# A hand-written order of TensorE's work in an attention stage, five probability row buffers and a shorter mask

## The chip, the cores and the metric

The kernel runs on one core of one Trainium2 chip. The metric is the device time of one execution in microseconds (us). Before the change it is 913.64 us, the median of three runs (912.99 to 913.8). The four engines that matter here are TensorE (PE in the rows, its weight loads PEld), VectorE (DVE), ScalarE (ACT) and SyncE (SP), which issues the DMAs.

## What is computed

A trunk of two layers over 1040 tokens (1024 frames behind 16 meta tokens), width 1024: first multi-head latent attention, then a gated linear recurrence, each with an output projection and a residual, and a last norm. The change touches the attention alone. Cut to what matters, for each of 8 heads:

```
s = (q_nope @ k_nope.T + q_rope @ k_rope.T) * scale     # 1040 x 1040
s = where(key <= query, s, -1e30)
p = softmax(s, axis=-1)
o = p @ v                                               # 1040 x 128
y = o * silu(gate)
```

All matrices are 32-bit. Each operand is split into a high and a low part (`hi_of` on ACT, `lo_of` on DVE), and a product is three matmuls: high by high, high by low, low by high (`mm3`).

## The kernel before, in words

**The stages.** The input norm, the latent projections, the gates and the rotary part of the queries come first. Then comes the attention (lines 420 to 699), from about 202 to 513 us of the span, then the output projection, the recurrence and its projection.

**The units of the attention.** Queries are cut into nine blocks of 116 rows (the last has 112), `QBLK`, line 43. A unit is one head and one block (h, t), and there are 72 of them. Three blocks make a group of 348 queries, `CH`. For each unit the program does the following, in this order.

- `scores(h, t)`, line 485: five matmuls for each piece of up to 512 keys, into a PSUM tile of two banks, `ps_2`. Block 0 to 2 have one piece, block 3 has one of 464 keys, blocks 4 to 7 have two, and block 8 has three (two in a first tile and one in a second one). There are two such tiles. Then DVE adds the mask and takes the row's minimum `m` (line 515, the queries carry the minus sign), ACT does the exponential into the row buffer `p` and the row's sum `l` (line 523), DVE the reciprocal (line 527), and DVE or, from block 6 on, ACT scales the row (lines 528 to 531). For block 8 the minimum is taken over both tiles (line 521) before either exponential.
- `transposes(h, t)`, line 534: TensorE transposes the row, 116 keys at a time, up to three into one PSUM tile `pt` (there are two of these, `nt[0] = 2`); ACT makes the high part `pth` of it (line 80) and DVE the low part `ptl` (line 83).
- `weighted(h, g)`, line 560: once for each group of three blocks, the transposed rows times `v`, into a PSUM tile of `ps_g`, and DVE multiplies by the gate into `Y` (line 574).

The k, q and v products of the coming head (`k_unit`, `q_unit`, `v_unit`) and the loads and splits of the next weights (`load_pair`, `part_out`) are handed out to units by the table `fill` (line 648 on). In the last head the places of the coming head's work are taken by the first tiles of the output projection (`part_out`, `a_out0`).

**What sets the order.** A main loop (line 686) records `scores` three units ahead (`LEAD = 3`), then `weighted`, then the unit's `fill`, then `transposes`. The recording is no order of execution: a scheduler orders each engine's instructions from its own plan of the time, and each engine then works through its list strictly in turn. So a row of transposes may stand in the middle of another product. `behind(marks, f)` holds f's instructions behind the given ones.

**Buffers.** Row buffers `p` are three of 1040 columns (line 496). The mask is 8 x 116 columns, zero but for a triangle at its end (line 424). [...]

**Names below.** s2_8_1 are the scores of head 2, block 8, tile 1; pt2_6_1 the second PSUM tile of transposes of head 2, block 6; o2_1 the weighted product of head 2, group 1; pk, pqn and pv the products of `k_unit`, `q_unit`, `v_unit`; kh, qh, wah, yh are high parts (ACT) and kl, ql, wal, yl low parts (DVE) of keys, queries, output weights and attention outputs; ao0_0 the first tile of the output projection. In ptl7_0_0 the numbers are head, group and tile, so its source tells the block.

Of the kernel before, what the change touches and what calls it, by code (L numbers as in the profile page):

```python
# [47 lines left out]
MASKW = 8 * QB  # L48
# [14 lines left out]
def trunk(ctx, tc, x, meta, a_norm_g, a_w_in, a_q_g, a_kv_g, a_w_uq, a_w_ukv, a_w_out,  # L63
# [20 lines left out]

    def mm3(ps, lh, ll, rh, rl, start, stop, **kw):
        nc.tensor.matmul(ps, lh, rh, start=start, stop=False, **kw)  # L86
        nc.tensor.matmul(ps, lh, rl, start=False, stop=False, **kw)  # L87
        return nc.tensor.matmul(ps, ll, rh, start=False, stop=stop, **kw)  # L88

    def mm_stack(ps, xp, k, n, wh, wl):  # L90
        if k:
            nc.tensor.matmul(ps[:n], xp[:, k, :n], wl, start=False, stop=False)
        nc.tensor.matmul(ps[:STK + n], xp[:, k], wh, start=k == 0, stop=k == KT - 1)
        if not k:
            nc.tensor.matmul(ps[:n], xp[:, k, :n], wl, start=False, stop=False)
# [41 lines left out]
    def rms_r(ms, n, w, name):  # L137
        v = sml.tile([P, w], F32, name=f"v_{name}", tag="rv")[:n]
        r = sml.tile([P, w], F32, name=f"r_{name}", tag="rr")[:n]
        t = sml.tile([P, w], F32, name=f"t_{name}", tag="rt")[:n]  # L140
        root = nc.scalar.activation(t, ms, AF.Sqrt, bias=eps[:n])
        nc.vector.tensor_scalar(v, ms, -0.5, -0.5 * EPS, ALU.mult, ALU.add)
        nc.vector.reciprocal(t, t)
        if w == 1:
            nc.vector.scalar_tensor_tensor(r, t, v, t, ALU.mult, ALU.mult)
        else:
            nc.vector.tensor_tensor(r, t, t, ALU.mult)
            nc.vector.tensor_tensor(r, r, v, ALU.mult)
        nc.vector.scalar_tensor_tensor(r, r, 1.5, t, ALU.add, ALU.mult)
        return r, root  # L150
# [16 lines left out]
    def transpose_in(xn, n, t0, xth, xtl, name):  # L167
        for j in range(2):
            pt = ps_t(f"xt_{name}_{j}")
            pv = pt.rearrange("p (a b) -> p a b", b=P)[:, :, :n]  # L170
            for a in range(4):
                k = 4 * j + a
                nc.tensor.transpose(pv[:, a], xn[:n, k * P:(k + 1) * P], ident[:n, :n])
# [97 lines left out]
    def lat_norm(i, pq, pk):  # L271
        t0, n = TOK[i]
        ms = sml.tile([P, 2], F32, name=f"lms{i}", tag="lms")[:n]
# [20 lines left out]
    def lat_post(i, lt, krf):  # L294
# [3 lines left out]
        for a in range(QKT):  # L298
            nc.tensor.transpose(pv[:, a], lt[:, a * P:(a + 1) * P], ident[:n, :n])
        nc.tensor.transpose(pv[:, 3], krf[:, 0:P], ident[:n, :n])  # L300
# [5 lines left out]
        for a in range(VKT):  # L306
            nc.tensor.transpose(pv[:, a], lt[:, QL + a * P:QL + (a + 1) * P], ident[:n, :n])
        nc.tensor.transpose(pv[:, 2], krf[:, DR:DR + P], ident[:n, :n])
# [19 lines left out]
    for c in range(0, D, 512):  # L328
        ps = ps_m(f"rb_ga{c}")
        nc.tensor.matmul(ps, ones, g_a[0:1, c:c + 512], start=True, stop=True)  # L330
# [98 lines left out]

    def load_pair(h):  # L430
# [10 lines left out]
    def k_unit(h, c):  # L441
# [6 lines left out]
        for k in range(VKT):  # L448
            last = mm3(ps, kvw[0][:, k, hh * 256:hh * 256 + DN], kvw[1][:, k, hh * 256:hh * 256 + DN],
                       klh[:, k, c0:c0 + cw], kll[:, k, c0:c0 + cw], k == 0, k == VKT - 1)  # L450
        kh, kl = KK[h]
        hi_of(kh[:, c0:c0 + cw], ps)
        lo_of(kl[:, c0:c0 + cw], ps, kh[:, c0:c0 + cw])
        return last
# [30 lines left out]
    def scores(h, t):  # L485
# [10 lines left out]
        p = pat.tile([QB, T], F32, name=f"p{h}_{t}", tag="p", bufs=3)[:n]  # L496
        pss = []
        a, b_, r_ = qh[:, off:off + n], ql[:, off:off + n], qr[:, off:off + n]
        for s, sg in enumerate(tiles):
            ps2 = ps_2(f"s{h}_{t}_{s}")  # L500
            w = sg[0][1]
            for j, (k0, w_) in enumerate(sg):
                assert w_ == w
                ps = ps2[:n, j, :w]
                nc.tensor.matmul(ps, a, kth[:, k0:k0 + w], start=True, stop=False)  # L505
                nc.tensor.matmul(ps, a, ktl[:, k0:k0 + w], start=False, stop=False)
                nc.tensor.matmul(ps, b_, kth[:, k0:k0 + w], start=False, stop=False)
                nc.tensor.matmul(ps, r_, ks1[:, k0:k0 + w], start=False, stop=False)
                nc.tensor.matmul(ps, r_, ks2[:, k0:k0 + w], start=False, stop=True)  # L509
            ns, k0 = len(sg), sg[0][0]  # L510
            pv = ps2[:n, :ns, :w]
            if s == len(tiles) - 1:
                lo = MASKW - QB - (ns * w - n)
                mk = maskt[:n, lo:lo + ns * w].rearrange("p (a b) -> p a b", a=ns)
# [3 lines left out]
            pss.append((pv, p[:, k0:k0 + ns * w].rearrange("p (a b) -> p a b", a=ns)))  # L518
        mx = m[:, 0:1]
# [14 lines left out]
    def transposes(h, t):  # L534
# [3 lines left out]
        p = PP.pop((h, t))  # L538
        if t % 3 == 0:
# [3 lines left out]
        for tr in range(g + 1):  # L543
# [4 lines left out]
            for j, kb in enumerate(kbs):  # L548
                k0, nk = QBLK[kb]
                nc.tensor.transpose(pv[:nk, j], p[:, k0:k0 + nk], ident[:n, :n])  # L550
# [98 lines left out]
    for h in range(H):  # L649
        for c in range(len(CH)):  # L650
# [3 lines left out]
            if u + 1 >= 0:  # L654
                fill[units[u + 1]].append(lambda h=h, c=c: q_unit(h, c))
# [15 lines left out]
    behind([silu], nc.scalar.activation, warm, ones[:, 0:1], AF.Exp)  # L671
    k_unit(0, 0)
    ku = k_unit(0, 1)
    behind([ku], q_unit, 0, 0)
    for u in range(-LEAD - 2, 0):
        for c in (1, 2):
            if 3 * c - LEAD - 2 == u and c > 1:
# [6 lines left out]
    for u in range(LEAD):  # L684
        scores(*units[u])
    for u, (h, t) in enumerate(units):
        if u + LEAD < len(units):
            scores(*units[u + LEAD])
        if pending:
            weighted(*pending)  # L690
            pending = None
        for f in fill[h, t]:
            f()
        transposes(h, t)
        if t % 3 == 2:
            pending = (h, t // 3)
    weighted(*pending)
# [299 lines left out]
    def late(i, c, done):  # L997
        ms = sml.tile([P, 1], F32, name=f"msb{i}", tag="msb", bufs=2)
        square(i, c, ms)
        v = sml.tile([P, 1], F32, name=f"v_f{i}", tag="rv")  # L1000
# [143 lines left out]
```

## Time and profile before

| | |
|---|---|
| median of three runs | 913.64 us |
| the profiled execution, its own time | 913.04 us |
| its span | 911.3 us |
| TensorE busy | 887.8 us, 97% of the span, 5291 matmuls |
| VectorE busy | 582.9 us, 64% |
| ScalarE busy | 467.7 us, 51% |
| GpSimd busy | 43.6 us, 5% |
| mean granted clock of TensorE | 0.997 |
| chain that ended last | TensorE 92%, ScalarE 3%, VectorE 2% |

A matmul's row is as long as it takes from its start to its end, and the next one starts before that end; so "busy" hides the spacing of starts, and a pause between two matmuls shows as idle time only from the end of the first.

### The profile page before, as it was taken

The numbers are of one execution on the slowest core, as the hardware profiler recorded it, in microseconds if no ns is written. First come the engines' busy times: TensorE is split into PE (matmuls) and PEld (weight loads), VectorE is DVE, ScalarE is ACT, GpSimd is POOL, SyncE is SP. The second block draws the span as 40 slices with busy tenths as digits, with TensorE's granted clock in tenths as the row PEclk, the third lists the DMA queues.
The fourth block names the chain that finished last, engine by engine and source line by source line (L and its number), as shares of the span: only waits on it lengthen the run. The fifth ranks groups of instructions, "written<-read, shape, count | busy, mean of one in ns | idle before, by whom it ended". The sixth has DMA issues, their size and how long they took to land.

```text
span 911.3 us, 13708 instructions
## 1 busy us (share of the span) xinstructions
PE 887.8 (97%) x5291; PEld 817.2 (90%) x5291; DVE 582.9 (64%) x1211; ACT 467.7 (51%) x942; POOL 43.6 (5%) x46
## 2 busy tenths in 40 slices
PE   7999999999999999999999999999999999999996
PEld 5999999999999999999988778799989989897885
DVE  6675423416677676676777357757393764868997
ACT  6543422224665655656656235634835457365455
POOL 3000000000000000000000000000020110312200
PEclk9999999999999999999999999999999999999998
DMA  7132345221010010010012424241111121237624
GB/s 275 48 87 64 85 110 158 73 72 40 16 57 16 17 55 16 17 63 16 17 37 103 163 92 159 101 75 48 46 47 51 43 58 36 95 90 231 141 68 184
DMA packets 71169, 72.25 MB, mean 79 GB/s; under 512 B 15056, under 2 KB 52688, under 8 KB 71104
## 3 DMA queue, kind: packets, MB, share of 16 engines
q1 hardware_dynamic: 68928, 67.19, 23.8%
q0 software_dynamic: 2176, 4.19, 2.6%
q8 instruction: 41, 0.67, 0.3%
q14 instruction: 24, 0.20, 0.1%
HBM read 58.65 MB, written 12.71 MB: 78 GB/s over the span
## 4 chain that ended last, share of the span: by engine, by line
PE 92%; ACT 3%; DVE 2%; issue 1%; DMA 0%; ACTq 0%; DVEq 0%
PE pt L550 4%; PE pu L88 3%; PE pu L86 3%; PE pu L87 3%; PE ga L86 3%; PE ao L86 3%; PE ga L87 3%; PE ga L88 3%; PE ao L88 3%; PE ao L87 3%; PE pg L87 3%; PE pg L88 3%; PE pg L86 3%; PE s L505 2%; PE b L86 2%; PE b L88 2%
## 5 line engine op out<-in xcount | busy, mean ns | idle before, releaser
L523 ACT ACTIVATE p<-s,m 116x116 f32<-116x116 f32 (+4 forms) x80 | 55.4, 694 | 45.1 <-DVE m L515 16.5
L80 ACT ACTIVATE pth<-pt 116x348 fp32r<-116x348 f32 (+5 forms) x152 | 57.1, 397 | 29.7 <-PE pt L550 26.2
L83 DVE TENSOR_TENSOR ptl<-pt,pth 116x348 fp32r<-116x348 f32 (+5 forms) x152 | 63.7, 437 | 9.7 <-ACT pth L80 9.2
L88 PE MATMUL pu<-x2h,l_wu 128*128 128x348 f32 (+1 forms) x192 | 61.5, 321 | 0.4 <-DVE l_wu L83 0.4
L86 PE MATMUL ga<-xth,h_wg 128*128 128x348 f32 (+1 forms) x192 | 61.9, 322 | 0.0
L86 PE MATMUL pu<-x2h,h_wu 128*128 128x348 f32 (+1 forms) x192 | 61.7, 322 | 0.0
L87 PE MATMUL pu<-x2l,h_wu 128*128 128x348 f32 (+1 forms) x192 | 61.7, 321 | 0.0
L87 PE MATMUL ga<-xtl,h_wg 128*128 128x348 f32 (+1 forms) x192 | 61.6, 321 | 0.0
L88 PE MATMUL ga<-xth,l_wg 128*128 128x348 f32 (+1 forms) x192 | 61.6, 321 | 0.0
L515 DVE CUSTOM_DVE_ANT_0 s<-s,maskt 116x116 f32<-116x116 f32 (+8 forms) x72 | 49.4, 686 | 16.9 <-PE s L509 16.6
L550 PE MATMUL pt<-ident,p 116*116 116x116 f32 (+1 forms) x360 | 54.0, 262 | 1.0 <-DVE ptl L83 0.6
L86 PE MATMUL ao<-wah,yh_a 128*128 128x512 f32 x128 | 50.5, 396 | 0.6 <-DVE Y L574 0.6
L87 PE MATMUL pg<-x2l,h_wbg 128*128 128x512 f32 x128 | 50.6, 395 | 0.0
L88 PE MATMUL pg<-x2h,l_wbg 128*128 128x512 f32 x128 | 50.3, 393 | 0.0
L86 PE MATMUL pg<-x2h,h_wbg 128*128 128x512 f32 x128 | 50.2, 392 | 0.0
L88 PE MATMUL ao<-wah,yl_a 128*128 128x512 f32 x128 | 50.2, 393 | 0.0
L87 PE MATMUL ao<-wal,yh_a 128*128 128x512 f32 x128 | 49.8, 390 | 0.0
L505 PE MATMUL s<-kh,qh 128*116 128x348 f32 (+7 forms) x120 | 42.0, 350 | 6.5 <-ACT p L523 6.5
L550 PEld LDWEIGHTS pt<-ident,p 116*116 116x116 f32 (+1 forms) x360 | 41.5, 135 | 4.0 <-PE pt L550 1.5
L87 PE MATMUL o<-ptl,v 116*128 116x348 f32 (+1 forms) x144 | 45.1, 313 | 0.0
L86 PE MATMUL o<-pth,v 116*128 116x348 f32 (+1 forms) x144 | 43.2, 300 | 0.8 <-ACT pth L80 0.8
L88 PE MATMUL o<-pth,v 116*128 116x348 f32 (+1 forms) x144 | 44.0, 305 | 0.0
(328 smaller groups left out, 2652.7 us busy)
## 6 DMA issues: line engine op xcount, KB each, us to landing
wg<-in_a_w_in SPq DMA_DIRECT2D x8, 512.0 KB, 3.9
wa<-in_a_w_out SPq DMA_DIRECT2D x8, 512.0 KB, 3.5
wu<-in_b_w_in SPq DMA_DIRECT2D x8, 512.0 KB, 4.0
wbg<-in_b_w_in SPq DMA_DIRECT2D x8, 512.0 KB, 4.0
hr<-hscr SPq DMA_DIRECT2D x8, 512.0 KB, 8.2
out_h<-hr SPq DMA_DIRECT2D x16, 256.0 KB, 2.1
x<-in_x SPq DMA_DIRECT2D x7, 512.0 KB, 3.5
wq<-in_b_w_out SPq DMA_DIRECT2D x6, 512.0 KB, 3.5
```

Source lines behind the costliest of these rows:

```text
L80: return nc.scalar.activation(dst, src, AF.Copy)
L83: return nc.vector.tensor_tensor(dst, src, bc(hi), ALU.subtract)
L86: nc.tensor.matmul(ps, lh, rh, start=start, stop=False, **kw)
L87: nc.tensor.matmul(ps, lh, rl, start=False, stop=False, **kw)
L88: return nc.tensor.matmul(ps, ll, rh, start=False, stop=stop, **kw)
L505: nc.tensor.matmul(ps, a, kth[:, k0:k0 + w], start=True, stop=False)
L515: MKD[h, t] = nc.vector.tensor_tensor_reduce(pv, pv, mk, 1.0, -NEG, ALU.add, ALU.min, m[:, s:s + 1])
L523: MK[h, t] = nc.scalar.activation(dst, pv, AF.Exp, bias=mx, scale=-1.0, accum_out=l[:, s:s + 1])
L550: nc.tensor.transpose(pv[:nk, j], p[:, k0:k0 + nk], ident[:n, :n])
```

## The change

In steps: (1) all of TensorE's instructions are issued through `pe_mm` and `pe_tr`, which keep the last one in `PE_LAST`; in the main loop every step is held behind it (`next_pe`), so that in the attention TensorE's list is the recorded order. (2) That order is: the first tile's scores of the unit three ahead; the third tile of transposes of the unit before (`back`, only of blocks 6 to 8); the weighted product that is pending; the unit's `fill`; the second tile's scores and the softmax; the first two tiles of transposes of this unit. `scores` is a generator for this, which stops between its tiles. In `fill`, `q_unit` goes to the front of its list. (3) The row buffers become five, of their own widths, by the table `PSLOT`. (4) The mask becomes 5 x 116 columns, read for several pieces with overlap (`mask_of`). (5) At the start, the first `k_unit` is followed by the first `q_unit` and only then by the second `k_unit`, and the table of the exponential is loaded behind the first high part of the keys. (6) Some buffers of single columns become two instead of four.

```diff
-MASKW = 8 * QB
+MASKW = 5 * QB
+PSLOT = (0, 1, 2, 3, 4, 1, 2, 3, 4)
...
+    PE_LAST = [None]
+
+    def pe_mm(*a, **kw):
+        PE_LAST[0] = nc.tensor.matmul(*a, **kw)
+        return PE_LAST[0]
...
-        v = sml.tile([P, w], F32, name=f"v_{name}", tag="rv")[:n]
+        v = sml.tile([P, w], F32, name=f"v_{name}", tag="rv", bufs=2)[:n]
...
+    def mask_of(n, ns, w):
+        m = maskt[:n, MASKW - QB - (w - n) - (ns - 1) * n:]
+        return bass.AP(m.tensor, m.offset, [m.ap[0], (n, ns), (1, w)])
...
-        p = pat.tile([QB, T], F32, name=f"p{h}_{t}", tag="p", bufs=3)[:n]
+        sl = PSLOT[t]
+        pw = max(QBLK[u][0] + QBLK[u][1] for u in range(NQB) if PSLOT[u] == sl)
+        p = pat.tile([QB, pw], F32, name=f"p{h}_{t}", tag=f"p{sl}", bufs=1)[:n]
...
             pss.append((pv, p[:, k0:k0 + ns * w].rearrange("p (a b) -> p a b", a=ns)))
+            if s + 1 < len(tiles):
+                yield
...
-    def transposes(h, t):
+    def transposes(h, t, trs):
...
-                fill[units[u + 1]].append(lambda h=h, c=c: q_unit(h, c))
+                fill[units[u + 1]].insert(0, lambda h=h, c=c: q_unit(h, c))
...
-    behind([silu], nc.scalar.activation, warm, ones[:, 0:1], AF.Exp)
-    k_unit(0, 0)
-    ku = k_unit(0, 1)
-    behind([ku], q_unit, 0, 0)
+    first_k = behind([silu], k_unit, 0, 0)
+    behind([first_k], nc.scalar.activation, warm, ones[:, 0:1], AF.Exp)
+    q_unit(0, 0)
...
+    def next_pe(f, *a):
+        behind([PE_LAST[0]], f, *a)
+
+    back = None
     for u, (h, t) in enumerate(units):
-        if u + LEAD < len(units):
-            scores(*units[u + LEAD])
+        sc = scores(*units[u + LEAD]) if u + LEAD < len(units) else iter(())
+        next_pe(next, sc, None)
+        if back:
+            next_pe(transposes, *back)
+            back = None
         if pending:
-            weighted(*pending)
+            next_pe(weighted, *pending)
             pending = None
+        end = u + 1 == len(units)
+        if end:
+            next_pe(transposes, h, t, range(2))
         for f in fill[h, t]:
-            f()
-        transposes(h, t)
+            next_pe(f)
+        next_pe(next, sc, None)
+        if not end:
+            next_pe(transposes, h, t, range(min(t // 3 + 1, 2)))
+        if t // 3 == 2:
+            back = (h, t, (2,))
         if t % 3 == 2:
             pending = (h, t // 3)
```

**TensorE where one head's scores pass to the next head's**, here from head 2 to head 3 (six such places follow the same pattern, one with each next head). Before, with 18 rows of o2_1 and six of pv1_7 between:

```order
L509 MATMUL s2_8_1_3450<-ks2_87,qr2_2_3324 112x344
L550 MATMUL pt2_6_0_3530<-ident_78,p2_6_3344 116x116
L550 MATMUL pt2_6_1_3536<-ident_78,p2_6_3344 116x116 x3
L86 MATMUL o2_1_3504<-pth2_1_0_3371,v1_0_3094 128x348
...
L88 MATMUL pv1_7_3559<-h_wkv2_2929,kll_94 116x256
L550 MATMUL pt2_6_2_3542<-ident_78,p2_6_3344 116x116
L505 MATMUL s3_0_0_3494<-kh3_3413,qh3_0_3473 116x116
```

and now:

```order
L89 MATMUL s2_8_1_3466<-ks2_87,qr2_2_3324 112x344
L93 MATMUL pt2_5_0_3479<-ident_78,p2_5_3294 116x116 x3
L93 MATMUL pt2_5_1_3485<-ident_78,p2_5_3294 116x116 x3
L89 MATMUL s3_0_0_3494<-kh3_3413,qh3_0_3460 116x116
...
L89 MATMUL o2_1_3504<-pth2_1_0_3371,v1_0_3094 128x348
...
L93 MATMUL pt2_6_0_3530<-ident_78,p2_6_3344 116x116 x3
L93 MATMUL pt2_6_1_3536<-ident_78,p2_6_3344 116x116 x3
L89 MATMUL s3_1_0_3545<-kh3_3413,qh3_0_3460 116x232
...
L93 MATMUL pt2_6_2_3555<-ident_78,p2_6_3344 116x116
```

The next head's first scores have moved up: between them and the last scores of this head stand six transposes, where four transposes, 18 matmuls of o2_1, six of pv1_7 and one more transpose stood.

**VectorE in the last head**, from the low part of the last queries on. Before:

```order
L586 TENSOR_TENSOR wal0_0_5629<-wa0_0_5626,wah0_0_5628 128x1024
L586 TENSOR_TENSOR wal0_1_5635<-wa0_1_5632,wah0_1_5634 128x1024
L515 ISA s7_6_0_5593,m7_6_5590<-s7_6_0_5593,maskt_2172 116x2x406
...
L83 TENSOR_TENSOR yl_a0_0_0_5726<-Y_1217,yh_a0_0_0_5725 128x512
L527 RECIPROCAL l7_5_5551<-l7_5_5551 116x1
L83 TENSOR_TENSOR ptl7_0_0_5513<-pt7_2_0_5584,pth7_0_0_5512 116x3x116
L586 TENSOR_TENSOR wal0_2_5641<-wa0_2_5638,wah0_2_5640 128x1024
```

and now:

```order
L604 TENSOR_TENSOR wal0_0_5629<-wa0_0_5626,wah0_0_5628 128x1024
L604 TENSOR_TENSOR wal0_1_5635<-wa0_1_5632,wah0_1_5634 128x1024
L531 ISA s7_6_0_5593,m7_6_5590<-s7_6_0_5593,maskt_2172 116x2x406
...
L545 RECIPROCAL l7_5_5551<-l7_5_5551 116x1
L604 TENSOR_TENSOR wal0_2_5641<-wa0_2_5638,wah0_2_5640 128x1024
L84 TENSOR_TENSOR ptl7_0_0_5513<-pt7_2_0_5584,pth7_0_0_5512 116x3x116
```

A third split of output weights now stands ahead of the low part of block 2's transposes, and one of the outputs (yl) has gone behind it. **TensorE** there, from the last scores of block 6 on, before:

```order
L509 MATMUL s7_6_0_5593<-ks2_87,qr7_2_5582 116x406
L505 MATMUL s7_7_0_5667<-kh7_5229,qh7_2_5578 116x464
...
L86 MATMUL o7_0_5608<-pth7_0_0_5512,v3_0_4910 128x348
L86 MATMUL ao0_0_5724<-wah0_0_5628,yh_a0_0_0_5725 128x512
...
L87 MATMUL o7_0_5608<-ptl7_0_0_5513,v3_0_4910 128x348
```

and now:

```order
L89 MATMUL s7_6_0_5593<-ks2_87,qr7_2_5582 116x406
L89 MATMUL o7_0_5608<-pth7_0_0_5512,v3_0_4910 128x348
L89 MATMUL o7_0_5608<-ptl7_0_0_5513,v3_0_4910 128x348
...
L93 MATMUL pt7_3_0_5654<-ident_78,p7_3_5464 116x116 x3
...
L89 MATMUL s7_7_0_5667<-kh7_5229,qh7_2_5578 116x464
```

The weighted product o7_0, whose second matmul reads that low part, follows block 6's scores at once, where ten matmuls of block 7's scores and twelve of ao0_0 stood between.

## Rows read from the trace of the kernel before

**Rows 1.** The page, busy time of the engines.

```profile
PE 887.8 (97%) x5291; PEld 817.2 (90%) x5291; DVE 582.9 (64%) x1211; ACT 467.7 (51%) x942; POOL 43.6 (5%) x46
```

**Rows 2.** Busy time by stretch: us, busy us of PE, PEld, DVE, ACT, POOL, clock, DMA.

```profile
202.00:215.00 13.00, 11.35 (x80) 10.88 (x79) 6.72 (x22) 7.14 (x18) 0.00 (x0) 1.00 0.30 84
215.00:470.00 255.00, 249.01 (x1739) 240.40 (x1738) 178.70 (x494) 150.39 (x378) 0.00 (x0) 1.00 0.09 28
470.00:515.00 45.00, 42.02 (x238) 36.09 (x237) 28.41 (x59) 23.48 (x47) 0.20 (x1) 1.00 0.30 107
```

**Rows 3.** PE's waits from 202 to 515: us in total, times, longest.

```profile
PE s L505 <- ACT p L523: 6.5, 9, 1.0
```

**Rows 4.** Timeline in head 1: start, us, engine, line, operation, [idle before <-releaser].

```profile
264.44 0.94 ACT L523 ACTIVATE p<-s,m 116x812 f32<-116x812 f32 x1 [2.70 <-issue]
...
266.74 0.32 PE L505 MATMUL s<-kh,qh 128*112 128x348 f32 x1
...
266.90 0.32 PE L506 MATMUL s<-kl,qh 128*112 128x348 f32 x1
...
267.54 0.66 PE L550 MATMUL pt<-ident,p 116*116 116x116 f32 x5
...
267.94 1.03 ACT L523 ACTIVATE p<-s,m 116x928 f32<-116x928 f32 x1 [0.56 <-PE pt L550]
268.87 0.19 ACT L523 ACTIVATION_READ_ACCUMULATOR p<-s,m 116x1 f32 x1
...
269.12 0.41 PE L505 MATMUL s<-kh,qh 128*112 128x344 f32 x1 [0.92 <-ACT p L523]
```

**Rows 5.** The same timeline, on from the last scores of head 1.

```profile
269.85 0.32 PE L509 MATMUL s<-ks,qr 128*112 128x344 f32 x1
...
270.20 0.53 DVE L515 CUSTOM_DVE_ANT_0 s<-s,maskt 112x344 f32<-112x344 f32 x1
...
270.82 0.16 DVE L521 TENSOR_TENSOR m<-m 112x1 f32<-112x1 f32 x1
...
271.38 0.84 ACT L523 ACTIVATE p<-s,m 112x696 f32<-112x696 f32 x1
```

**Rows 6.** Groups by line and form, 215 to 470: busy us, mean ns | idle before.

```profile
L83 DVE TENSOR_TENSOR ptl<-pt,pth 116x348 fp32r<-116x348 f32 x63 | 32.1, 517 | 6.7 <-ACT pth L80 6.6
L80 ACT ACTIVATE pth<-pt 116x348 fp32r<-116x348 f32 x63 | 28.4, 461 | 16.7 <-PE pt L550 16.4
```

**Rows 7.** Timeline in the last head, from the high part of the last queries.

```profile
473.64 0.46 ACT L465 ACTIVATE qh<-pqn 128x344 fp32r<-128x344 f32 x1 [1.61 <-PE pqn L88]
...
474.00 2.00 ACT L80 ACTIVATE wah<-wa 128x1024 fp32r<-128x1024 f32 x2
...
475.08 2.36 DVE L586 TENSOR_TENSOR wal<-wa,wah 128x1024 fp32r<-128x1024 f32 x2 [0.43 <-ACT wah L80]
...
477.36 1.00 DVE L515 CUSTOM_DVE_ANT_0 s<-s,maskt 116x812 f32<-116x812 f32 x1
477.38 0.47 PE L505 MATMUL s<-kh,qh 128*116 128x464 f32 x1 [0.96 <-ACT p L523]
...
478.28 0.69 DVE L83 TENSOR_TENSOR yl_a<-Y,yh_a 128x512 fp32r<-128x512 f32 x1
...
478.95 0.50 DVE L83 TENSOR_TENSOR ptl<-pt,pth 116x348 fp32r<-116x348 f32 x1
```

**Rows 8.** Timeline at the start of the attention.

```profile
203.67 1.28 ACT L317 ACT_TABLE_LOAD   x1
...
205.53 0.95 DVE L83 TENSOR_TENSOR kl<-pk,kh 128x348 fp32r<-128x348 f32 x2 [1.23 <-ACT kh L80]
206.11 0.43 PE L86 MATMUL pqn<-qlh,h_wq 128*128 128x348 f32 x1 [1.65 <-DVE kl L83]
```

**Rows 9.** Busy time by stretch after TensorE's last matmul, columns as rows 2.

```profile
904.00:906.00 2.00, 0.00 (x0) 0.00 (x0) 1.85 (x7) 1.63 (x6) 0.00 (x0) 1.00 0.60 224
906.00:908.00 2.00, 0.00 (x0) 0.00 (x0) 1.34 (x5) 0.80 (x2) 0.00 (x0) 0.60 0.63 236
```

More of the change, by code (lines that the diff above doesn't have):

```diff
@@ L172, in transpose_in @@
                 k = 4 * j + a
-                nc.tensor.transpose(pv[:, a], xn[:n, k * P:(k + 1) * P], ident[:n, :n])
+                pe_tr(pv[:, a], xn[:n, k * P:(k + 1) * P], ident[:n, :n])
             hs = xth[:, 4 * j:4 * j + 4, t0:t0 + n]
@@ L272, in lat_norm @@
         t0, n = TOK[i]
-        ms = sml.tile([P, 2], F32, name=f"lms{i}", tag="lms")[:n]
+        ms = sml.tile([P, 2], F32, name=f"lms{i}", tag="lms", bufs=2)[:n]
         lt = pa1.tile([P, QL + KVL], F32, name=f"lt{i}", tag="lt", bufs=2)[:n]
@@ L298, in lat_post @@
         for a in range(QKT):
-            nc.tensor.transpose(pv[:, a], lt[:, a * P:(a + 1) * P], ident[:n, :n])
-        nc.tensor.transpose(pv[:, 3], krf[:, 0:P], ident[:n, :n])
+            pe_tr(pv[:, a], lt[:, a * P:(a + 1) * P], ident[:n, :n])
+        pe_tr(pv[:, 3], krf[:, 0:P], ident[:n, :n])
         hi_of(qlh[:, :, t0:t0 + n], pv[:, :3])
@@ L306, in lat_post @@
         for a in range(VKT):
[L307 to L308 removed]
+            pe_tr(pv[:, a], lt[:, QL + a * P:QL + (a + 1) * P], ident[:n, :n])
+        pe_tr(pv[:, 2], krf[:, DR:DR + P], ident[:n, :n])
         hi_of(klh[:, :, t0:t0 + n], pv[:, :2])
@@ L329, in trunk @@
         ps = ps_m(f"rb_ga{c}")
-        nc.tensor.matmul(ps, ones, g_a[0:1, c:c + 512], start=True, stop=True)
+        pe_mm(ps, ones, g_a[0:1, c:c + 512], start=True, stop=True)
         rbs.append(ps)
@@ L504, in scores @@
                 ps = ps2[:n, j, :w]
[L505 to L509, printed above, removed]
+                pe_mm(ps, a, kth[:, k0:k0 + w], start=True, stop=False)
+                pe_mm(ps, a, ktl[:, k0:k0 + w], start=False, stop=False)
+                pe_mm(ps, b_, kth[:, k0:k0 + w], start=False, stop=False)
+                pe_mm(ps, r_, ks1[:, k0:k0 + w], start=False, stop=False)
+                pe_mm(ps, r_, ks2[:, k0:k0 + w], start=False, stop=True)
             ns, k0 = len(sg), sg[0][0]
@@ L537, in transposes @@
         off = b0 - CH[g][0]
-        p = PP.pop((h, t))
-        if t % 3 == 0:
+        p = PP[h, t]
+        if t % 3 == 0 and 0 in trs:
             PT[h, g] = [(pat.tile([QB, GRP, CHW], F32R, name=f"pth{h}_{g}_{tr}", tag="pth", bufs=3),
@@ L542, in transposes @@
                         for tr in range(g + 1)]
-        for tr in range(g + 1):
+        for tr in trs:
             pth, ptl = PT[h, g][tr]
@@ L549, in transposes @@
                 k0, nk = QBLK[kb]
-                nc.tensor.transpose(pv[:nk, j], p[:, k0:k0 + nk], ident[:n, :n])
+                pe_tr(pv[:nk, j], p[:, k0:k0 + nk], ident[:n, :n])
             nfull = sum(1 for kb in kbs if QBLK[kb][1] == QB)
@@ L999, in late @@
         square(i, c, ms)
-        v = sml.tile([P, 1], F32, name=f"v_f{i}", tag="rv")
+        v = sml.tile([P, 1], F32, name=f"v_f{i}", tag="rv", bufs=2)
         r = sml.tile([P, 1], F32, name=f"r_f{i}", tag="rr")
```

29 lines of the change are left out of this document (16 added, 13 removed).

## The prediction

> **What bounds the kernel now.** I read the page first: TensorE is busy 97% of the span, no other engine over 64% [rows 1]. So a change that removes no work can only win pauses of TensorE, and it loses where it adds some. Then the busy time by stretch: in the attention, 202 to 515 us, TensorE stands idle 1.65 + 5.99 + 2.98 = 10.6 us [rows 2]. A matmul of 348 columns starts 0.16 us after the one before, but its row lasts 0.32 us [rows 4], so each pause is some 0.16 us longer than the idle time that it shows; the timeline has 23 pauses over 0.1 us: one at the start (before 206.11 [rows 8]), 15 in heads 0 to 6 (the largest before 269.12 [rows 4]), seven in the last head (the largest before 477.38 [rows 7]). Together 10.6 + 23 x 0.16 = **14.3 us**: 1.8, 8.4 and 4.1. That is all that any order can win here.
>
> Next the waits: 6.5 us of the idle time are scores that wait for an exponential to free their PSUM tile [rows 3]. The timeline says why it is late. At 264.44 ACT begins block 6's exponential after 2.70 us of nothing shown ("issue"): with three row buffers it must wait for the transposes of block 3. At 267.94 the next exponential starts when transposes end (named on the row), and the scores behind it start 0.92 us late [rows 4]. Five row buffers take exactly this wait away, since block 6 then follows block 2, whose transposes are long done.
>
> [...] By loads the idle time of the three stretches is 313 - 287.4 = 25.6 us [rows 2], and all of it won would turn the sum below into 918. I keep to the pauses between starts: the rows that make loads look idle are wide matmuls that follow each other without a pause.
>
> **What is gone.** All 14.3 us, counted as if every old pause vanished; what comes instead is counted anew. The mask, the widths of the row buffers and the buffers of single columns cost nothing: the same elements are read, and GpSimd fills the mask while 95% idle [rows 1]. On SP's queue two query loads pass ahead of a weight load that is needed three heads later; nobody waits.
>
> **What comes, term by term.** TensorE now works strictly in the written order, so each wait stops all that is queued behind it. I walked each engine's new list with the durations of the rows.
>
> (a) *From head to head, 7 times.* The next head's first scores need the PSUM tile of block 8's first tile. Its exponential needs the minimum over both tiles, so it starts only after the scores of the second one. Count from the start of the last of these matmuls [rows 5]: the mask starts at 0.35, the minimum at 0.97, the exponential could start at 1.16; its 0.84 and the hand-over (row 1.03, start to release 1.18 [rows 4], so 0.15 more) release the tile at 2.15. TensorE has one matmul interval (0.16) and six transposes at 0.10 (five last 0.66, of which 0.26 is the last one's length [rows 4]) to do: 0.76. That is a pause of 1.4 us at least. But ACT's list has the two high parts of those six transposes ahead of the exponential; at 0.46 each [rows 6], overlapping by 0.1, they end 1.5 to 1.6 after zero. Pause **1.7**, times 7 = **11.9 us**. Ends: 1.4 (9.8 in all) and 2.3 (16), where ACT is also late with block 7's row. The 18 matmuls of the weighted product, ready, stand behind this wait.
>
> (b) *Third tile of transposes, blocks 6 and 7, 7 heads.* There are two pt tiles, so the third needs the first one's low part: 0.26 + 0.46 + 0.52 [rows 6] and three hand-overs of 0.04 = 1.36 us from its last transpose. In between stand one interval, three transposes and the next head's scores: 0.10 + 0.30 + 0.55 = 0.95 for block 6 (five of 232 columns, in proportion), 1.19 for block 7, 1.45 for block 8. Pauses 0.4, 0.3 (0.17, and 0.15 since the keys' parts stand ahead on ACT and DVE) and none: 0.7 x 7 = **5.1 us**; ends 0 and 7.
>
> (c) *The first weighted product of odd heads, 3 times:* the next pair's query weights (768 columns, 0.9 us in proportion to [rows 7]) and two other jobs stand on DVE ahead of the low part it reads: 0.5 each, **1.4 us**; ends 0 and 3.
>
> (d) *The last head, weighted product o7_0.* In the trace 5.8 us pass from the high part of the last queries (473.64) to the end of block 2's low part (478.95 + 0.50) [rows 7]; TensorE spent them on the scores of blocks 6 and 7, a pause of about 1.1 before 477.38, and output tiles. Now a third split (2.36 / 2 = 1.2) stands ahead on DVE and 0.7 (yl) has gone behind: 6.3 us. TensorE has three transposes, ten matmuls of 406 columns (1.86) and one of o7_0 to do, 2.3 us, of which 0.2 lie before 473.64's counterpart: pause 6.3 - 2.1 = **4.2 us**; ends 3.5 and 5.
>
> (e) *The rest of the last head.* The same pt wait as in (b), with more ahead of it: 1.4 at block 4 (DVE is still behind from (d)), 1.0 at o7_1, which follows block 5's transposes at once (0.46 + 0.52 [rows 6] and the mask), 1.3 at block 6 (ACT's scaling of the 1040-column row), 2.3 at blocks 7 and 8, whose five tiles of transposes follow each other through two PSUM tiles, 0.8 at the end as before: **6.8 us**; ends 3 and 8.
>
> (f) *The start.* The high part of the keys no longer waits for the 1.28 us table load [rows 8], and the second key product stands behind the query product: **0.6 us** of small pauses are left of 1.8; ends 0.3 and 1.5.
>
> Sum: 11.9 + 5.1 + 1.4 + 4.2 + 6.8 + 0.6 = 30.0 against 14.3, so +15.7. The profiled execution took 913.04, so 928.7; the median of the runs lies 0.6 above it. **Forecast 929.3 us**, 1.7% slower.
>
> **Rivals.** *Only the pauses with a floor stay.* The pauses in (a) give ACT and DVE time, so they are ahead everywhere else: (a) 9.8, (b) 1.2, (c) 0, (d) 4.2, (e) 3, (f) 0.3 = 18.5. That is +4.2, 917.8 by the median. For it: both engines are idle 30 to 40% of the middle [rows 2]. Against: the splits in (d) stand in both lists whatever was idle earlier.
>
> *Faster.* The new boundary sits at its floor, and its time off is enough that DVE and ACT have the last head's splits done early, so that (d) vanishes and (e) keeps only the last 0.8: 9.8 + 0.8 + 0.3 = 10.9, or 3.4 less than now, 910.2 us. It decides once everything beside (a) is below 14.3 - 9.8 - 1.8 = 2.7 us. For it: the row-buffer waits do go. Against: the splits stand behind the last queries' high part in both orders [rows 7], and (b) is bound by 1.36 us of work that nobody can hide.
>
> *The clock falls.* After TensorE's last matmul (it ends near 903.9) the granted clock is full to 906 and a mean 0.60 in the next 2 us [rows 9]: idle, it fell to its lower level there. In (d) TensorE stands about 4 us with one matmul in the middle. [...] Against: the idle time in (d) is in two pieces of some 2 us, and the 0.96 us of idle time before 477.38 [rows 7] left the clock at 1.00 [rows 2]. [...]
>
> *It does not do what it says.* The pins could leave the lists as they were. The built lists contradict it; what could still be is that pauses only move, at 913 to 914.
>
> **How the numbers follow.** Forecast 0.65, floor rival 0.15, clock 0.11, faster 0.05, no change 0.04. A measurement of this kernel can tell 0.2%, 1.8 us, from no change; so faster is 0.05, same 0.04, slower 0.91. With all terms at their lower ends the sum is +2.3 (915.9), with all upper ends +26; since they hardly err together, I take 916 to 936. It holds the forecast with its bounds, most of the floor rival and the clock.
>
> **What would show it.** In the changed profile: (a) seven pauses of the next head's first scores, released by an exponential, 1.4 to 2.3 us apart from the transposes ahead of them; (b) 14 short waits of transposes for a low part; (d) one pause of over 3 us (in two pieces) in o7_0, released by the low part on DVE; ACT's wait "issue" ahead of the exponential gone; the middle of the attention with more idle time of TensorE than 10.6 us. I am wrong if TensorE's idle time from 202 to the end of the attention falls, or if the first scores of a head start right behind the transposes: then the tile is released earlier than I read from the lists.

## The result, and the profile after

The changed kernel took **943.0 us** (median of four runs; 941.22 and 942.72 in two later sets) against 913.37 of the kernel before: ratio 1.0313 (over all runs of both, not of the two medians), 95% interval 1.0268 to 1.0358. It is 29.6 us slower; 15.7 were forecast, and the time lies above the range.

The profiled execution took 936.54 us, the fastest of its four runs, at a mean granted clock of 0.999; the other three took 941.9 to 945.6 at 0.987 to 0.990. So the profile shows only part of the loss. First that part. The page's busy times of the changed kernel, against [rows 1]:

```profile
PE 894.7 (96%) x5291; PEld 816.0 (87%) x5291; DVE 583.0 (62%) x1211; ACT 468.4 (50%) x942; POOL 43.3 (5%) x46
```

The work is the same and the busy times differ by less than 1%: the loss is idle time. The same kernel's busy time by stretch, columns as in [rows 2]:

```profile
202.00:215.00 13.00, 12.60 (x85) 11.73 (x85) 7.05 (x22) 7.44 (x18) 0.00 (x0) 1.00 0.30 85
215.00:470.00 255.00, 236.34 (x1618) 222.90 (x1617) 167.91 (x459) 141.41 (x355) 0.00 (x0) 1.00 0.09 27
470.00:536.00 66.00, 57.89 (x350) 50.62 (x348) 38.55 (x89) 32.52 (x71) 0.20 (x1) 1.00 0.19 64
```

The start is better (0.4 us idle, 1.65 before), the middle three times worse: 18.7 us idle where it was 6.0. TensorE's waits in the changed kernel from 202 to 536 us (us in total, times, longest), against [rows 3]:

```profile
PE s L89 <- ACT p L541: 10.0, 7, 1.4
PE pt L93 <- DVE ptl L84: 5.2, 12, 1.2
PE s L89 <- DVE ql L481: 2.9, 7, 0.6
PE s L89 <- ACT qh L480: 2.7, 4, 0.8
PE o L89 <- ACT pth L81: 2.0, 2, 1.7
PE o L89 <- DVE ptl L84: 1.6, 2, 1.5
PE pk L89 <- DVE v L84: 0.9, 3, 0.3
```

Nine waits of up to 1.0 us for an exponential have become seven of 1.4, one between every two heads, and six kinds of wait stand below it that were small or absent: before, the rows under [rows 3] were 1.7 us at the start and 0.8, 0.6 and 0.6. The timeline at the end of head 1 shows one of the seven:

```profile
271.27 0.47 PE L89 MATMUL s<-ks,qr 128*112 128x344 f32 x2
...
271.49 0.52 DVE L481 SCALAR_TENSOR_TENSOR ql<-pqn,qh 128x348 fp32r<-128x348 f32 x1 [0.73 <-ACT qh L480]
271.59 0.76 PE L93 MATMUL pt<-ident,p 116*116 116x116 f32 x6
...
271.93 0.51 DVE L531 CUSTOM_DVE_ANT_0 s<-s,maskt 112x344 f32<-112x344 f32 x1
272.08 0.81 ACT L81 ACTIVATE pth<-pt 116x348 fp32r<-116x348 f32 x2 [0.62 <-PE pt L93]
...
272.54 0.16 DVE L539 TENSOR_TENSOR m<-m 112x1 f32<-112x1 f32 x1
...
272.78 0.84 ACT L541 ACTIVATE p<-s,m 112x696 f32<-112x696 f32 x1
...
273.77 0.31 PE L89 MATMUL s<-kh,qh 128*116 128x116 f32 x1 [1.42 <-ACT p L541]
```

Six transposes start at 271.59, 0.10 us apart; the next head's first scores start at 273.77. Between is the chain mask, minimum, exponential, with the two high parts on ACT just ahead of the exponential. Start to start, less the usual interval, that is a pause of 1.59 us, seven times 11.1. Added up over 202 to 545 us in this way, the pauses over 0.12 us make **35.4 us** (14.3 before): +21.1 of the 23.5 us between the two profiled executions. Of the other 2.4, 0.7 were lost before the attention (the last gate product starts at 202.93 in place of 202.22), 0.4 behind it (391.9 us from the last weighted product to the last matmul of the kernel, 391.5 before), and 1.3 in gaps under that size.

### The profile page after: what moved, and what is told of

It reads as the page before. It is cut to its first block, busy times and chain, and to the rows that moved or that the text cites. A ratio compares the mean times of both kernels' runs of the same rounds, so it can differ in the third digit from the quotient of the medians.

```text
span 934.8 us, 13627 instructions
## 1 busy us (share of the span) xinstructions
PE 894.7 (96%) x5291; PEld 816.0 (87%) x5291; DVE 583.0 (62%) x1211; ACT 468.4 (50%) x942; POOL 43.3 (5%) x46
## 4 chain that ended last, share of the span: by engine, by line
PE 84%; DVE 7%; ACT 6%; DMA 1%; issue 1%; ACTq 0%; DVEq 0%
PE ao L89 10%; PE pu L89 10%; PE ga L89 9%; PE s L89 8%; PE pg L89 8%; PE b L89 7%; PE o L89 6%; PE pz L89 5%; PE pk L89 5%; PE pq L89 3%; PE pqn L89 3%; PE pt L93 3%; PE qr L89 2%; PE pv L89 2%; ACT p L541 2%; DVE ptl L84 1%
## 5 line engine op out<-in xcount | busy, mean ns | idle before, releaser
L89 PE MATMUL o<-pth,v 116*128 116x344 f32 (+5 forms) x288 | 65.4, 305 | 2.0 <-ACT pth L81 2.0
L89 PE MATMUL s<-ks,qr 128*116 128x348 f32 (+7 forms) x240 | 58.4, 324 | 0.0
L89 PE MATMUL s<-kh,qh 128*116 128x348 f32 (+7 forms) x120 | 43.9, 366 | 12.7 <-ACT p L541 10.0
L89 PEld LDWEIGHTS o<-pth,v 116*128 116x128 f32 (+1 forms) x288 | 49.5, 189 | 2.6 <-ACT pth L81 2.6
L93 PEld LDWEIGHTS pt<-ident,p 116*116 116x116 f32 (+1 forms) x360 | 39.2, 135 | 13.0 <-DVE ptl L84 11.1
```

The lines of the kernel that those rows point to most:

```text
L89: PE_LAST[0] = nc.tensor.matmul(*a, **kw)
L93: PE_LAST[0] = nc.tensor.transpose(*a)
```

## Experiments

Each run stands beside runs of the kernel before on its chip. "Pauses" are counted in the profile of the run as above. The letters B to G, M and P name theories; each is told in the expected text where it first comes up.

**again.** No edit. 

> The changed kernel once more, to catch the profile of a usual run: the first profile fell on the fastest run (936.5 us, mean granted clock 0.999) while the other three took 942 to 946 at 0.987 to 0.990. Theory C (the clock falls in the last head): median 942 to 945, and a profile of a run at about 0.99 shows the same 35 us of pauses as the first one, and a stretch of granted clock well under 1.00 that begins in or right behind the pauses of the last head (490 to 520 us); some 7 us of the time lie there. Rival M (it falls in the middle, at the pauses from head to head): the stretch lies before 480 us. Rival P (not the clock): the pauses themselves are longer by 7 us and the clock's difference is spread thin.

Measured: 941.22 us, just under C's 942, ratio 1.0315 (1.0285 to 1.0344), runs at 0.987 to 0.994. Its profiled run (938.70) caught two falls of the clock. Busy time by stretch of this run, columns as in [rows 2]:

```profile
312.00:314.00 2.00, 0.76 (x8) 0.53 (x5) 1.92 (x6) 1.50 (x4) 0.00 (x0) 1.00 0.32 87
314.00:315.50 1.50, 1.32 (x10) 1.32 (x11) 0.52 (x4) 0.84 (x5) 0.00 (x0) 1.00 0.00 1
315.50:319.00 3.50, 3.50 (x17) 3.50 (x16) 0.45 (x2) 1.32 (x3) 0.00 (x0) 0.51 0.00 0
319.00:322.00 3.00, 2.72 (x23) 2.53 (x23) 2.44 (x8) 1.90 (x6) 0.00 (x0) 1.00 0.00 0
```

After the pause of 1.59 us TensorE works again from 314.18, at a clock of 1.00, and some 1.4 us later the clock goes to 0.50 for 3.5 us. Matmuls of 348 columns start 0.16 us apart ahead of the fall (314.96, 315.12) and 0.29 us apart in it (316.17, 316.46). At 0.51 these 3.5 us do 1.7 us less work than at 1.00. The busy share hides it: PE reads 3.50 of 3.50. The second fall, 500.0 to 503.5, follows the pauses in o7_0. So C and M each hold for one of the two. P does not: the seven pauses are 1.59 us here too, and the rest are as in the first profile.

**tailfree.** The order in the last head is left to the list scheduler:

```
     def next_pe(f, *a):
-        behind([PE_LAST[0]], f, *a)
+        behind([PE_LAST[0]] if pin[0] else [], f, *a)
...
+        pin[0] = u < (H - 1) * NQB + 2
```

> The changed kernel with the written order ended after block 1 of the last head, so that the rest of this head stands as the list scheduler puts it. Theory C: the 9.6 us of pauses in the last head shrink to about 4 (they were 4.1 in the kernel before), and with them the clock stays up: median 929 to 933, mean granted clock 0.997. Rival M: only the pauses go, the clock still falls in most runs: 936 to 940. If the last head costs nothing beyond its pauses and these come back elsewhere: 942.

Measured: 933.57 us (931.07 to 935.96), ratio 1.0218 (1.0195 to 1.0240), between the ranges of C (929 to 933) and M (936 to 940). The last head's pauses are 4.5 us, 5 fewer, as C and M both have it. But the clock went on falling: 0.992 to 0.999, and the profile has falls at 352, 472 and 530 us, the first two 1.4 and 1.6 us after the end of a pause of 1.59 from head to head, the third 2.4 us after the end of one of 1.48 in the last head. C's place for the clock is wrong; it falls in the middle as well.

**q_early.** The third query product one block earlier:

```
-                fill[units[u + 1]].insert(0, lambda h=h, c=c: q_unit(h, c))
+                fill[units[max(u + (c != 2), 0)]].insert(0, lambda h=h, c=c: q_unit(h, c))
```

> The changed kernel with the query product of the third group put one block earlier, so that the scores of block 6 no longer follow it at once. Theory C with the walk: the waits for the two parts of the queries at the scores of block 6 go (1.75 us in three heads, 0.4 to 0.6 in five: 7.4 us in the first profile), a little of it comes back where the product now stands: 5 to 7 us less, median 935 to 938, the clock as often down as before. Rival (the wait moves to the next thing in line): within 2 us of the changed kernel.

Measured: 940.31 us, ratio 1.0279 (1.0245 to 1.0312): the rival, within 2 us. The waits for the queries' parts go, but the scores now wait for the keys' low part right behind the key product (2.8 us in three waits) and value products for a PSUM tile of products (2.4 in four): start to start, 7.6 us of pauses went and 6.4 came. The profiles show this and the medians do not, since falls of the clock blur them: this profile (941.09) has six, four behind pauses of 1.59 and two in the last head, that of again two. Where this product moved, the wait for its evacuation moved with it; what could still hide it was work between it and its reader.

**rows5.** The kernel before with `PSLOT`, its five row buffers, the short mask and the smaller single columns, and nothing else. 

> The kernel before with the five row buffers, the short mask and the smaller buffers of single columns alone; the order is the list scheduler's. Theory C: the buffers are not what costs; ACT's exponentials no longer wait for a row buffer, the scores' waits of 6.5 us shrink to 1 to 3: 908 to 912. Rival B (the buffers' places or the mask cost something themselves): 915 or more. Third way (the scheduler's order changes with the buffers, and the waits only move): 912 to 915.

Measured: 914.51 us over ten runs, ratio 1.0012 (1.0002 to 1.0021): the third way. TensorE's waits for an exponential do shrink; this row of the run's waits, 202 to 515 us, answers to [rows 3]:

```profile
PE s L512 <- ACT p L529: 2.2, 5, 0.6
```

But the pauses only fall from 14.3 to 12.9 us: many of 0.1 to 0.7 us, for parts of queries and keys, for transposed tiles and in the last head, come instead. The buffers by themselves bring nothing and cost 0.2% at most. The loss is in the order.

**boundary.** The order from head to head alone:

```
+        if t == 6 and pending:
+            next_pe(weighted, *pending)
+            pending = None
         next_pe(next, sc, None)
+        if t == 5:
+            next_pe(transposes, h, t, range(2))
...
-        if not end:
+        if not end and t != 5:
             next_pe(transposes, h, t, range(min(t // 3 + 1, 2)))
```

> The changed kernel with another order from head to head alone: the transposes of block 5 ahead of the second tile of block 8's scores, and the 18 matmuls of the weighted product ahead of the next head's first scores. The profiles of the run again and of the two others have each a few stretches of some 3.5 us at granted clock 0.50, most of them 3 to 5 us after a pause of 1.59 us from head to head, each costing some 1.7 us. Theory D (pauses of some 1.6 us let the clock fall now and then): the seven pauses go (11.1 us) and with them the falls in the middle; what is left is falls at the last head's pauses: 925 to 931, and no granted clock under 1.00 between 215 and 470 us. Theory C of before (only the last head's pauses let it fall): 931 and the falls elsewhere as before. Rival (the tile's release is late for another reason than the order, so the wait comes back at the next scores): 937 or more.

Measured: 931.47 us (930.37 to 932.39), ratio 1.0186 (1.0171 to 1.0202), half a microsecond above D's range. The seven pauses are gone; 1.24 us came back in three heads, between the two transposed tiles of block 5, and some smaller ones. In head 1 the tile is released by a low part at 269.13, ahead of which on DVE stands the minimum of block 8's first tile (0.88 us from 268.33); no split of the next pair's weights is near, though the text expected for spread puts the wait down to them. The run's busy time by stretch, columns as in [rows 2]:

```profile
215.00:470.00 255.00, 241.06 (x1656) 226.98 (x1655) 167.83 (x468) 142.59 (x363) 0.00 (x0) 1.00 0.09 27
...
490.00:492.50 2.50, 0.45 (x2) 0.21 (x2) 2.50 (x6) 2.50 (x5) 0.00 (x0) 0.98 0.81 282
492.50:499.30 6.80, 6.80 (x24) 5.95 (x25) 4.06 (x9) 2.42 (x6) 0.00 (x0) 0.51 0.59 200
```

No fall in 255 us of the middle, and one where the last head's two pauses stand, this time 6.8 us long. That is D, and the other runs at 0.994 to 0.998 agree.

**covered.** The order of boundary, tailfree's free last head, the third group's key and query products ahead of their block's scores, block 6's and 7's third transposed tile behind the first job of its step, and in odd heads one value product behind the keys' product:

```
+        if t in (1, 2):
+            next_pe(fs.pop(0))
...
+        if back and t > 6 and fs:
+            next_pe(fs.pop(0))
```

> A version that covers each pause of the changed kernel's profile with work: the order from head to head as in the run boundary; the keys' and queries' products of the third group ahead of the scores of their block; the third tile of transposes behind the first job of its block; in odd heads one value product behind the keys' product; and the written order ended after block 1 of the last head. Theory D: of 35.4 us of pauses there remain some 0.7 at the start, 4 to 5 in the last head and 1 to 3 elsewhere, against 14.3 before, and none is long enough for the clock: 904 to 909, faster than both. Rival (waits move to the next thing in line, as in the run with the early query product): 912 to 918. If the clock falls without long pauses: over 918.

Measured: 918.87 us, ratio 1.0052 (1.0039 to 1.0064); the clock stayed at 0.997 to 0.999. That is far outside D's range (904 to 909), and 0.9 us above that of the rival. Pauses 18.1 us; transposes that wait for a low part are idle for 7.6 us of them. D's price per pause held (3.7 us more pauses than before, 4.7 us more time), its guess of what would remain did not: waits that had stood behind others came up, as the rival has it.

**spread.** Heads 0 to 6 as one list per head, so that every two transposed tiles have work between them; the last head free as in tailfree, with block 5's transposes and the weighted product placed as in boundary; NEARLY 5 in place of 3, with two more output tiles in the last head:

```
+        s8 = scores(h, 8)
+        steps += [(next, s8, None), (transposes, h, 5, (0,)), (q_unit, n, 0), (transposes, h, 5, (1,)),
+                  (next, s8, None), (transposes, h, 6, (0,)), (weighted, h, 1), (transposes, h, 6, (1,)),
+                  (sc_all, n, 0), (transposes, h, 6, (2,)), (sc_all, n, 1), (v_unit, vn, va),
+                  (transposes, h, 7, (0,)), (k_unit, n, 1), (transposes, h, 7, (1,)), (sc_all, n, 2),
...
```

> A second written order, from the pauses left in the run covered (18.1 us: 1.24 in three heads where a transposed tile waits behind the splits of the next pair's weights, 0.4 to 0.7 where products follow each other through two PSUM tiles, 1.48 + 0.77 at the end of the last head). In heads 0 to 6 every two tiles of transposes have some work between them, the weights of the next pair are loaded one block earlier, and two more tiles of the output product stand in the last head, one behind its last weighted product. Theory D (the time is the sum of the pauses, plus the clock where one of them is long): 1 us at the start, 0 to 2 in heads 0 to 6, 2 to 3 in the last head, 4 to 6 in all against 14.3 before: 903 to 906, faster than before by 0.9 to 1.2%. Rival (each wait only moves, as in the run with the early query product): 912 or more, with as many pauses in other places.

Measured: **903.44 us** (902.99 to 903.78), ratio **0.9889** (0.9872 to 0.9905): 1.1% faster than before and 4% faster than the changed kernel, at the place that D gives. The run's busy time by stretch, columns as in [rows 2]:

```profile
202.00:215.00 13.00, 12.60 (x84) 11.49 (x82) 7.06 (x22) 7.49 (x18) 0.00 (x0) 1.00 0.29 85
215.00:470.00 255.00, 254.64 (x1787) 246.70 (x1788) 184.19 (x505) 157.83 (x392) 0.21 (x1) 1.00 0.10 31
470.00:515.00 45.00, 43.71 (x234) 37.29 (x233) 24.40 (x51) 18.87 (x39) 0.00 (x0) 1.00 0.29 100
```

TensorE is idle 0.4 us in 255. Of 14.3 us of pauses before, 3.7 are left; the time fell by 10.4.

**spread_pause.** The run spread, with the changed kernel's order from head to head:

```
+        steps += [(next, s8, None), (q_unit, n, 0), (next, s8, None), (transposes, h, 5, (0,)),
+                  (transposes, h, 5, (1,)), (sc_all, n, 0), (weighted, h, 1), (transposes, h, 6, (0,)),
+                  (transposes, h, 6, (1,)), (sc_all, n, 1), (v_unit, vn, va), (transposes, h, 6, (2,)),
```

> The run spread with the changed kernel's order from head to head put back, and that alone: the next head's first scores right behind the transposes of block 5, which follow the scores of block 8, and the weighted product behind them. It measures the pause from head to head by itself, with nothing else that is long before the last head. Theory D: seven pauses of 1.6 us (11.1 us) and, behind some of them, a stretch at granted clock 0.50 of 3 to 4 us that costs 1.7 us each; with 2 to 5 of them 14 to 20 us above the run spread, runs that differ by more than 2 us among themselves, mean granted clock 0.990 to 0.995. Rival (the clock needs the last head's pauses too): 11 us above spread, with the runs as close together as those of before.

Measured: 918.74 us (917.38 to 920.0), 15.3 above spread, ratio to before 1.0055 (1.0040 to 1.0071). The seven pauses of 1.59 are back, and seven of 0.46 at a transposed tile. Together they are 14.3 us of the 15.3; so the time lies in D's range, but not for D's reason. The clock hardly fell: 0.996 to 0.998, with no fall in the profile, where two to five falls and 0.990 to 0.995 were expected. This missed.

**changed_same_chip.** No edit. 

> The changed kernel a third time, beside the runs spread_pause and spread_long on the same chip. The run spread_pause had the seven pauses of 1.59 us, yet its granted clock stayed at 0.996 to 0.998, where the changed kernel's runs went down to 0.987. Theory E (each such pause lets the clock fall only by chance, and chips differ in how often): on one chip both kernels fall about as often per pause; if the changed kernel is at 0.99 here, spread_pause is at or under 0.994 too, the changed kernel having one more place, the last head. Theory F (the other pauses of the changed kernel, 0.3 to 1 us within 20 us, are needed as well): the changed kernel at 0.987 to 0.994 and 939 to 945 us, spread_pause again at 0.996 or more.

**spread_pause_same_chip.** No edit. 

> The run spread_pause again (the order spread with the changed kernel's order from head to head put back), for the same chip as the changed kernel. Theory E: 918 to 925, granted clock 0.990 to 0.996 wherever the changed kernel is down as well. Theory F: 917 to 920 at 0.996 to 0.998, as before.

Measured: the changed kernel 942.72 us at 0.987 to 0.993, ratio 1.0313 (1.0298 to 1.0329), the other 920.18 us with all runs at 0.995, ratio 1.0069 (1.0052 to 1.0086). The profiles have two falls behind seven pauses of 1.59 us in the first and one in the second. This lies between E and F, nearer to F: E wants 0.994 or less in the second, F 0.996 or more and 917 to 920. But F does not hold by itself either: tailfree has the changed kernel's middle with all its smaller pauses, and ran at 0.992 to 0.999. What makes the changed kernel fall more often is left open.

**spread_long.** The run spread, with the next head's first scores right behind block 8's:

```
-                  (next, s8, None), (transposes, h, 6, (0,)), (weighted, h, 1), (transposes, h, 6, (1,)),
-                  (sc_all, n, 0), (transposes, h, 6, (2,)), (sc_all, n, 1), (v_unit, vn, va),
+                  (next, s8, None), (sc_all, n, 0), (transposes, h, 6, (0,)), (weighted, h, 1), (transposes, h, 6, (1,)),
+                  (transposes, h, 6, (2,)), (sc_all, n, 1), (v_unit, vn, va),
```

> The run spread with the next head's first scores put right behind the second tile of block 8's scores, with no transposes between: the pause from head to head is then the whole chain mask, minimum, exponential and release, 2.15 us, less one matmul interval: 2.0 us seven times. Pauses alone: 903.4 + 14 = 917 to 918. Theories E and F alike: a longer pause lets the clock fall more often than one of 1.59 us; at 1.7 us for each fall 920 to 930, granted clock 0.987 to 0.996. If length does not matter: as often as spread_pause in the same call, 918 to 920.

Measured: 928.38 us (926.05 to 929.14), ratio 1.0151 (1.0136 to 1.0166), clock 0.987 to 0.990. The first of the seven, in the run's busy time by stretch (columns as in [rows 2]):

```profile
235.00:237.50 2.50, 0.43 (x3) 0.13 (x1) 1.47 (x5) 1.16 (x4) 0.00 (x0) 1.00 0.25 70
237.50:241.00 3.50, 3.48 (x15) 3.48 (x16) 1.39 (x7) 2.21 (x6) 0.00 (x0) 0.52 0.00 0
241.00:244.00 3.00, 3.00 (x27) 3.00 (x26) 1.00 (x3) 0.76 (x3) 0.00 (x0) 0.99 0.02 5
```

The pause is 2.25 us, and six of the seven are followed by such a stretch. The profiled run (929.14) is 26.0 above that of spread (903.12); 15.8 are the pauses, so 10.2 remain for six falls, 1.7 each: the price of 3.5 us at 0.52. A fall came more often behind the longer pause: six times in seven here, and on the same chip once in seven behind 1.59 us in spread_pause (0.995). Counted over seven profiles (the changed kernel's three, tailfree, q_early, spread_pause twice) a pause of 1.59 us was followed by one 10 times in 49, four of them in q_early's profile alone.

**spread_rows3.** The run spread with the old row buffers:

```
-        p = pat.tile([QB, pw], F32, name=f"p{h}_{t}", tag=f"p{sl}", bufs=1)[:n]
+        p = pat.tile([QB, T], F32, name=f"p{h}_{t}", tag="p", bufs=3)[:n]
```

> The run spread with the three row buffers of the kernel before, each as wide as all keys, in place of the five: are the buffers worth anything under a good order? Theory D: an exponential then waits for the transposes three blocks earlier, which stand behind its scores in the written order; the scores two blocks on and the boundary feel it: some 1 us in blocks 6 to 8 of each head, 908 to 912. Rival G (the order alone does it): within 1.8 us of the run spread, 902 to 905.

Measured: 903.62 us (902.44 to 904.14), ratio 0.9892 (0.9876 to 0.9909), and TensorE busy 255.00 of 255 us in the middle: the rival. With work between the transposed tiles three row buffers were enough here, and D's row-buffer waits did not come.

## Why the prediction was wrong

The sign was right, and so was the kind of cause: waits in a strict order stop all that is queued behind, as at 273.77, where the matmuls of the weighted product (from 274.32 on) stand behind the pause of 1.59 us. The size was wrong by 13.7 us (943.0 against 929.3): 5.4 are pauses missed (35.4 against 30.0), 6.5 the distance of the median from the profiled run (943.0 against 936.5), which is the clock (an estimate from the mean clocks, 0.999 against 0.987 to 0.990, since the profile is of the fastest run alone), and 1.8 the 2.4 us outside the counted pauses less the 0.6 that the forecast added. Two steps failed. Step (c) was 7.5 us too small (1.4 for 7.6 at its true place and 1.3 at one not walked), and the other terms together 2.1 too large. And the clock was weighed for (d) alone and left out of the sum.

*What is gone, the old 14.3 us, and (f).* Right: the old waits are gone or counted anew, and the start has 0.7 for 0.6.

*(a) From head to head.* Right: 1.59 for 1.7, 11.1 us for 11.9. Both high parts on ACT ahead of the exponential are in the timeline, as the step had them, but they cost less than the 0.3 us added for them. Counted from the last matmul of the scores (271.43), the exponential starts at 1.35 where the step's floor has 1.16. Of these 0.19 us, 0.14 come from DVE, which the step took as free: the low part of the next head's queries (271.49) is ahead of the mask, so the mask starts at 0.50 for 0.35 and the minimum at 1.11 for 0.97. The run boundary shows the term by removing it.

*(b) Third transposed tile.* Right: 0.43 and 0.30 in seven heads, 5.1 us for 5.1 (the step's 0.7 x 7 is 0.73 x 7).

*(c) The first weighted product of odd heads.* This is **the step that failed** in the walk. It saw the next pair's query weights on DVE ahead of a low part, but followed them to the wrong reader. The changed kernel's timeline in head 1:

```profile
258.64 0.84 ACT L81 ACTIVATE h_wq<-wq 128x768 fp32r<-128x768 f32 x1 [0.83 <-PE pqn L89]
...
259.39 0.44 ACT L480 ACTIVATE qh<-pqn 128x344 fp32r<-128x344 f32 x1
259.69 0.95 DVE L84 TENSOR_TENSOR l_wq<-wq,h_wq 128x768 fp32r<-128x768 f32 x1
...
259.88 0.44 PE L89 MATMUL s<-kh,qh 128*116 128x406 f32 x1 [0.82 <-ACT qh L480]
...
260.56 0.51 DVE L481 SCALAR_TENSOR_TENSOR ql<-pqn,qh 128x344 fp32r<-128x344 f32 x1
...
261.12 0.45 PE L89 MATMUL s<-kh,ql 128*116 128x406 f32 x1 [0.61 <-DVE ql L481]
```

The weights' high part (0.84) stands on ACT ahead of the queries' high part, their low part (0.95) on DVE ahead of the queries' low part. The next reader is the scores of block 6, which the written order puts three transposes behind the query product: 0.98 + 0.77 us in odd heads, 0.4 to 0.6 in even ones and the last, 7.6 us in all. By the time of the first weighted product the wait is over: the 1.4 us of the step are not there. A value product after two others, and so a key product that waits for their PSUM tile (`ps_g` has two), 0.45 in three heads, was not walked at all. The list of TensorE's waits in the kernel before has no row of either kind.

*(d) o7_0.* Right in place and kind: 1.90 + 1.73 = 3.6 us for 4.2, in two pieces. The second is released by the low part, behind a weight split on DVE:

```profile
495.62 0.43 PE L89 MATMUL o<-pth,v 116*128 116x348 f32 x1 [1.74 <-ACT pth L81]
...
495.81 1.21 DVE L604 TENSOR_TENSOR wal<-wa,wah 128x1024 fp32r<-128x1024 f32 x1
...
496.93 0.52 DVE L84 TENSOR_TENSOR ptl<-pt,pth 116x348 fp32r<-116x348 f32 x1
...
497.50 0.42 PE L89 MATMUL o<-ptl,v 116*128 116x348 f32 x1 [1.46 <-DVE ptl L84]
```

*(e) The rest of the last head.* 6.0 us for 6.8, with each wait within 0.3 us of the one named.

*The clock.* This is the other step that failed. It stood among the rivals at 0.11, with one place, (d), and was argued away there since a pause of some 1 us had left it at 1.00. In the runs a fall lasted about 3.5 us at 0.50 and cost some 1.7 us, and (d) was not its only place: it fell behind (a)'s pauses of 1.59 us as well, as tailfree (falls in the middle with a short last head) and boundary (none without those pauses) show from two sides, and there are seven of them. The step compared (d) with one pause of before (0.96 us of idle time) and did not ask the same of (a), whose 1.7 us lie above every pause in the middle of before (1.08 at most). To ask would not have settled it: the pause at the start of the attention of before, 1.65 us of idle time ahead of 206.11 [rows 8] and 1.81 from start to start, left the clock at 1.00 [rows 2]. One pause without a fall proves little, as 1.59 us went without one in 39 of 49 cases.

*The rivals of a floor and of a gain* needed (b) and (e) to shrink, and the gain (d) as well; (b) was 5.1, (d) 3.6 and (e) 6.0 us. *The loads as measure:* the run spread was idle 0.4 us by matmuls and 8.3 by loads in the middle, and its gain, 10.4 us, is the 10.6 us of pauses it removed. For this kernel the pauses between starts were the measure.

*Costs set to nothing* (mask, row widths, single columns): right to within 0.2%, by rows5.

## What to carry to other kernels

When an order is written out by hand for an engine that is 97% busy, list for each product, evacuation or chain on the other engines its next reader in the new order, and put work of at least that length between; transposed tiles, PSUM tiles of products and parts of queries each needed it here (waits of up to 1.2, 0.3 and 0.8 us in the changed kernel), and in q_early 7.6 us of uncovered waits became 6.4 us at the next in line. Walk each late instruction to its first reader, not to the one you have in mind. Here a pause cost its length (14.3 us more of pauses, 15.3 us more time in spread_pause), and behind one of 1.48 us or more the clock could fall, for some 1.7 us on top: one long pause that the old trace shows without harm (1.81 us here) does not clear a new one that comes once in every head, since 1.59 us was followed by a fall in 10 of 49 cases only.

## What was not expected of the hardware

A pause of 1.59 us was followed by a fall to 0.50 of the granted clock in 10 of 49 cases, one of 2.25 us in 6 of 7. The falls behind pauses of 1.59 began 1.3 to 1.9 us after the pause had ended (not 3 to 5, as the text expected for boundary has it), so they showed in the rows when TensorE was busy again. Each lasted about 3.5 us (6.8 once, behind two pauses of 1.9 and 1.7 us in a row). In the middle of the attention of the profiles of before, rows5, boundary, covered and spread, where no pause is over 1.3 us, the clock stayed at 1.00; but in the last head a pause of 1.48 us was followed by a fall in tailfree, and the pauses of 1.81 and 1.82 us at the start of the attention in before and rows5 were not.

Which pause is hit changes from run to run: of the seven, none in the first profile of the changed kernel, one in again (the fall at 315.6 us), two in changed_same_chip (394.7 and 473.2). Runs of the changed kernel spread over 9 us (936.5 to 945.6) where those of before lie within 2 in each comparison, and its fastest run was the one with the profile: a single profile at 0.999 showed nothing of it, and only the mean clock of the other runs did. Why the changed kernel falls more often in a run than spread_pause, with the same seven pauses, is not settled: tailfree, with its middle, ran at 0.992 to 0.999, boundary, with its last head, at 0.994 to 0.998, and the changed kernel at 0.987 to 0.994 in 11 of 12 runs.
